# A planned decoder kernel: start loads, sample block, turned loops and planner model changed together

## The chip, the cores and the metric

The kernel runs as one program on the 8 cores of one Trainium2 chip: cores 0 to 3 are one die, 4 to 7 the other. The metric is the device time in microseconds (us) of the slowest core. Executions fall in a fast and a slow state; in the slow one the cores of a die show a lower granted TensorE clock (down to about 0.81 of full) and the time is some per cent, for the kernel before up to 18%, longer.

## The reference, cut to what matters

```python
def mixer_layer(h, p_i, ...):                       # 4 layers, D_MODEL = 1024, D_FF = 2816
    z = rmsnorm(h, g_mix) @ w_in                    # columns: A (xa, gate_b, gate_c), B (u, v), C (c_in)
    ...
    y_a = gate_b * causal_dwconv(gate_c * xa)       # 3 taps
    y_b = gelu(u) * chunk_spatial_mix(layernorm(gelu(v)))
    y_c = silu(layernorm(causal_dwconv(glu(c_in)))) # 31 taps
    h = h + concat(rmsnorm(y_a), rmsnorm(y_b), rmsnorm(y_c)) @ w_out
    f = rmsnorm(h, g_ffn)
    h = h + (silu(f @ w_gate) * (f @ w_up)) @ w_down
    gate = sigmoid(rmsnorm(h, g_ple) @ w_ple_gate)  # per-layer input embedding
    return h + gate * (p_i @ w_ple_proj)
```

Each core has one prompt of 2048 rows and 128 rows of samples. Four RMS norms a layer stand in the path of the matmuls: each needs the whole row's sum of squares before the first matmul behind it can have its input.

## The kernel before

The rows are worked through in two halves of 1024, each in two blocks of 512 columns; the sample block of 128 columns rides with the first half. So the four layers of the first half have three blocks and those of the second half two. A layer reads its weights from HBM anew in each half: wC, wV, wU, wA and wT for the mixing stage, wO for the output projection, wF and wD for the feed-forward pair, wP for the embedding.

The kernel is a graph of operations. A list scheduler fixes in advance, from a cost model, the order of the instructions on every engine, and also every address in SBUF.

```python
    for o in reversed(ops):                         # plan(): latest start D of each operation
        ...
        if o.dma:
            o.D = dend - (o.dma / 120.0 + 500)
        ...
            if o.dma:                               # two queues modelled as independent
                q = "sw" if e == "pool" else "hw"
                b0 = max(dmaf[q], t + o.cost + 900)
                dmaf[q] = b0 + o.dma / 125.0
                o.end = dmaf[q] + 1100
```

A norm: ScalarE squares the eight chunks of h into buffers SQ (two buffers of four chunks), VectorE or GpSimd adds them, TensorE sums over the partitions with a matrix of ones, ScalarE takes the root (RB), VectorE scales the eight chunks one by one into NRM.

```python
    def norm(H, bi, n, gcol, label="NRM", dt=BF16):
        bank = sumsq(H[bi], n)                      # SQ, additions, ones-matmul
        rb = rstd(bank, n, 1.0 / D)                 # RB
        dst = keys8(label, bi, n, dt)
        scale_by(H[bi], gcol, rb, dst, n)           # eight scalar_tensor_tensor, NRM
        return dst
```

The matmuls behind a norm take one PSUM bank at a time and all eight chunks for it, so the first of them waits for the last chunk:

```python
            for m in range(8):                      # wO; c_proj, wF and wP are built alike
                ps = G.psum(n)
                pe(n, mmg(lambda ps=ps: ps.ap, [(..., lambda k=MX[bi][kc]: k.ap) for kc in range(8)]),
                   [w] + MX[bi], (ps,))
                residual(bi, m, ps)
```

The order in which the parts of the mixing stage enter the graph is given by strings (Q = C projection, V, U, A, K, L, M = mixing, a, b, c = group norms; the last digit is the block), one for each half and one for the very first layer.

Of the kernel before, what the change touches and what calls it, by code (L numbers as in the profile page):

```python
# [11 lines left out]
DEPTH = 4  # L12
# [12 lines left out]
RING = 65536  # L25


SEQ = ("Q1 A00 Q2 Q0 A01 K0 A02 K1 V1 L0 V0 L1 A20 A12 B A10 U2 U0 c1 c0 M0 V2 L2 a0 c2 b0 A21 U1 A11 M1 a1 A22 M2 b2 b1 a2",
       "A00 V1 Q0 Q1 K1 A10 V0 K0 L1 U0 L0 A20 B A21 a0 M0 b0 c0 A01 U1 M1 c1 A11 b1 a1")
SEQ_FIRST = "R* K0 A0* B K1 M* L0 b0 A10 A20 c0 a0 L1 b1 A11 A21 c1 a1 L2 b2 A12 A22 c2 a2"  # L30
# [10 lines left out]
def c_pe(n):  # L41
    return max(n / 2.4 + 3.0, 58.0)
# [44 lines left out]
class Op:  # L87
    __slots__ = ("i", "eng", "cost", "fn", "deps", "raw", "succ", "tiles", "tset", "T", "D", "start", "end", "pos",
                 "dma", "sem", "val", "ndep", "est", "waits", "snap", "needed", "count", "wslab", "gate", "pre", "bg", "alt")


class Graph:
# [24 lines left out]
    def op(self, eng, cost, fn, r=(), w=(), tset=None, dma=0, gate=None, slab=None, bg=False, alt=None):  # L117
        o = Op()
        o.alt = alt or {}
# [33 lines left out]
    def plan(self, nunits, verbose=False):  # L153
# [9 lines left out]
        for o in reversed(ops):  # L163
# [16 lines left out]
            if o.dma:  # L180
                o.D = dend - (o.dma / 120.0 + 500)
            elif o.eng == "pe":
                o.D = min(o.T, dend - o.cost * 1.1)
            else:
                o.D = dend - o.cost * 1.3 - 100
# [7 lines left out]
        def takes(o, e, t):  # L193
# [5 lines left out]
            return t + o.alt[e][0] <= busy + o.cost  # L199
# [7 lines left out]
        dmaf = {"sw": 0.0, "hw": 0.0}  # L207
# [72 lines left out]
        while done < total:  # L280
# [4 lines left out]
            for e in ENGS:  # L285
# [3 lines left out]
                for o in ready[e]:  # L289
# [13 lines left out]
                    for tl in o.tiles:  # L303
                        if tl.at > a:
                            a = tl.at
                    cands.append((a, o))
# [81 lines left out]
            if o.dma:  # L388
                q = "sw" if e == "pool" else "hw"
                ft[e] = t + o.cost  # L390
                b0 = max(dmaf[q], t + o.cost + 900)
                dmaf[q] = b0 + o.dma / 125.0
                o.end = dmaf[q] + 1100
            else:
# [8 lines left out]
                o.end = t + c  # L403
            o.pos = len(order[e])
# [105 lines left out]
def build_program():  # L510
# [94 lines left out]
    def dve(n, fn, r, w, rate=1.0, ptr=0, flex=False, alt=None):  # L605
        alt = dict(alt or {})
        if flex:
            alt["pool"] = (c_pool(n), fn)
        return G.op("dve", c_dve(n, rate, ptr), fn, r, w, alt=alt)
# [10 lines left out]
    def load(out, in_, nbytes, w, gate=90000, r=()):  # L620
        return G.op("sp", 60, lambda e: e.dma_start(out=out(), in_=in_), r, w, dma=nbytes, gate=gate)
# [4 lines left out]
    def cast_load(out, in_, nbytes, w, gate=90000):  # L626
        return G.op("pool", 900, lambda e: e.dma_start(out=out(), in_=in_), (), w, dma=nbytes, gate=gate)

    def slab(label, src, n, after=()):
        k = Key(G, Tile(label, "w", n * 2), 0, n, BF16)  # L630
        G.op("pool", 600, lambda e: e.dma_start(out=k.ap, in_=src), after, (k,), dma=128 * n * 2, slab=k.tile)  # L631
# [7 lines left out]


    G.op("sp", 60, lambda e: e.dma_start(out=VECT[:], in_=vec), (), (kVEC,), dma=128 * NV * 4)
# [17 lines left out]
    def keys8(label, bi, n, dt):  # L659
        if n == 512:  # L660
# [61 lines left out]
    def ld_x(hf, blocks, bi, after=()):  # L722
# [3 lines left out]
        if kind == "S":  # L726
            load(lambda: G.whole(h).ap.rearrange("p (k t) -> p k t", k=8), xv[:, :, r0:r0 + n], 128 * n * 32, h)
# [5 lines left out]
    def layer(hf, l, blocks, H, NRM):  # L733
        nb = len(blocks)
        BI = range(nb)

# [13 lines left out]
        if hf == 0:  # L750
# [15 lines left out]


        kC = [slab("wC", wC[l, j], 2048) for j in range(2)]
        first = hf == 0 and l == 0
        kVl = []  # L770

        def wV_():
            if not kVl:
                kVl.append(slab("wV", wV[l], 3072, after=H[0] if first else ()))
            return kVl[0]
        if first:
            wV_()
            H[1] = ld_x(hf, blocks, 1, after=(kC[1],))
            NRM[1] = norm(H, 1, 512, lambda c: vcol(0, 0, c))
        wk = {}  # L780

        def wU_():
            if "U" not in wk:
                wk["U"] = slab("wU", wU[l], 3072)
            return wk["U"]
# [575 lines left out]
```

## Time and profile before

| | before |
|---|---|
| time, median of 4 runs | 3319.58 us |
| fast runs | 3318.25 to 3320.47 us |
| spans by core, profiled run | die 0 3310.2 to 3315.3 us, die 1 3293.7 to 3302.4 us |
| granted clock by core | 0.986 to 0.988 |
| core 2: TensorE idle | 3315.3 - 3163.3 = 152.0 us |
| core 2: first matmul of wO, first layer | 151.4 us |
| core 2: last layer of the first half, first wP matmul to the second half's first wO | 1712.3 to 1868.0, 155.7 us |

Columns of a list of what ended the idle time: us in total, times, longest.

```profile
PE PS L637 <- POOL SQ L689: 7.7, 3, 3.2
...
PE PS L637 <- DMA wO<-wO: 0.4, 1, 0.4
```

The wait for wO is there on all cores of die 0 (7.4 to 13.9 us) and nearly absent on die 1 (0 to 2.0 us). It is most of the 17 us between cores 2 and 7: their four stretches from the first wO to the first wF matmul in the second half add up to 135.0 and 120.6 us. That holds for this execution only. In the fast runs of the same kernel on two other chips, die 0 was the slower one in four of seven.

### The profile page before, as it was taken

How to read it: one execution, taken by the hardware profiler on the slowest of the kernel's cores; microseconds unless marked ns; L12 is line 12 of the kernel's file. 1: busy time of each engine (PE TensorE's matmuls, PEld its weight loads, DVE VectorE, ACT ScalarE, POOL GpSimd, SP SyncE). 2: the span in 40 equal slices, each digit the busy share in tenths (PEclk: the TensorE clock that was granted, in tenths of full speed). 3: DMA queues.
4: the chain of work that ended last, by engine and by line, in shares of the span. 5: the costliest groups of instructions: out<-in, count | busy, mean ns of one | idle time of the engine just before them, and what ended most of it. 6: DMA issues, size and time to landing. Idle time of an engine off the chain costs nothing.

```text
span 3315.3 us, 45695 instructions; the slowest of 8 cores (3293.7 to 3315.3 us)
## 1 busy us (share of the span) xinstructions
PE 3163.3 (95%) x18278; PEld 1549.7 (47%) x18278; DVE 1664.8 (50%) x2910; ACT 1182.8 (36%) x2052; POOL 537.0 (16%) x694
## 2 busy tenths in 40 slices
PE   4899999999999999999988899999999999999998
PEld 2455545555455554555544344444444444444443
DVE  4842179522696215972149721495117831386116
ACT  3631157311473113641125511363115621264114
POOL 4200033000331002310022200130002200031000
PEclk9999999999999999999999999999999999999999
DMA  9734545535365353753633745338443574428431
GB/s 176 117 64 71 87 69 99 102 55 88 57 113 92 59 89 59 117 87 62 124 70 95 114 82 100 67 49 139 83 85 70 83 122 89 81 48 131 79 58 51
DMA packets 75054, 288.78 MB, mean 87 GB/s; under 512 B 14304, under 2 KB 24672, under 8 KB 59488
## 3 DMA queue, kind: packets, MB, share of 16 engines
q0 software_dynamic: 47808, 255.09, 46.4%
q1 hardware_dynamic: 27040, 30.77, 3.1%
q8 instruction: 151, 2.47, 0.3%
q14 instruction: 55, 0.45, 0.1%
HBM read 529.55 MB, written 12.78 MB: 164 GB/s over the span
## 4 chain that ended last, share of the span: by engine, by line
PE 77%; DVE 14%; DMA 4%; ACT 2%; issue 2%; POOL 0%; SPq 0%; DVEq 0%; ACTq 0%; POOLq 0%
PE PS L637 77%; DVE NRM L709 2%; DMA wO<-wO 2%; DVE MX L709 1%; DVE TMP L1172 1%; DVE ACC L1028 1%; DVE H L1174 1%; DVE H L1112 1%; ACT SQ L666 1%; DMA nap<-XAP 1%; DVE TMP L1053 1%; DMA H<-xin 1%; DVE SQ L684 1%; DVE Y L951 0%; ACT L1206 0%
## 5 line engine op out<-in xcount | busy, mean ns | idle before, releaser
L637 PE MATMUL PS<-NRM,wF 128*128 128x512 bf16 x5632 | 1224.7, 379 | 3.5 <-DVE NRM L709 3.5
L637 PEld LDWEIGHTS PS<-NRM,wF 128*128 128x128 bf16 x5632 | 548.8, 98 | 657.6 <-issue 5.4
L1139 DVE TENSOR_TENSOR HID<-TMP,PS 128x512 bf16<-128x512 f32 x352 | 242.1, 688 | 930.8 <-PE PS L637 930.5
L637 PE MATMUL PS<-HID,wD 128*128 128x512 bf16 x2816 | 612.8, 379 | 0.0
L1137 ACT ACTIVATE TMP<-PS 128x512 f32<-128x512 f32 (+1 forms) x440 | 234.5, 533 | 1013.6 <-PE PS L637 1013.5
L666 ACT ACTIVATE SQ<-H 128x512 bf16<-128x512 f32 x416 | 253.0, 626 | 732.1 <-DVE H L1112 608.6
L637 PEld LDWEIGHTS PS<-HID,wD 128*128 128x128 bf16 x2816 | 274.7, 98 | 327.5
L1112 DVE TENSOR_TENSOR H<-H,PS 128x512 f32<-128x512 f32 x256 | 174.8, 685 | 479.9 <-PE PS L637 479.7
L709 DVE SCALAR_TENSOR_TENSOR NRM<-H,VEC,RB 128x512 bf16<-128x512 f32 x384 | 287.9, 803 | 18.1 <-ACT RB L670 17.7
L637 PE MATMUL PS<-NRM,wA 128*128 128x512 bf16 x1152 | 269.5, 388 | 3.0 <-DVE NRM L709 3.0
L637 PE MATMUL PS<-MX,wO 128*128 128x512 bf16 x1024 | 234.8, 389 | 10.4 <-DMA wO<-wO 7.4
L637 PE MATMUL PS<-NRM,wP 128*128 128x512 bf16 x1024 | 235.5, 381 | 9.2 <-DVE NRM L709 9.2
L1206 ACT ACT_TABLE_LOAD x162 | 207.8, 1283 | 2.5
L637 PEld LDWEIGHTS PS<-NRM,wA 128*128 128x128 bf16 x1152 | 112.9, 100 | 140.3 <-issue 14.7
L637 PEld LDWEIGHTS PS<-MX,wO 128*128 128x128 bf16 x1024 | 101.4, 100 | 137.5 <-issue 25.9
L637 PEld LDWEIGHTS PS<-NRM,wP 128*128 128x128 bf16 x1024 | 100.5, 98 | 130.9 <-issue 12.2
L637 PE MATMUL PS<-SQ,ONES 128*128 128x512 bf16 (+1 forms) x210 | 62.4, 359 | 93.6 <-DVE SQ L698 58.0
L631 POOL DMA_DIRECT2D wF<-wF x88 | 48.4, 552 | 591.0 <-PE PS L637 589.0
L631 POOL DMA_DIRECT2D wD<-wD x64 | 33.9, 532 | 672.6 <-PE PS L637 657.2
L637 PE MATMUL PS<-NRM,wC 128*128 128x512 bf16 x512 | 116.7, 385 | 7.1 <-DVE BST L873 7.1
L684 DVE TENSOR_TENSOR SQ<-SQ 128x1024 bf16<-128x1024 bf16 (+1 forms) x121 | 76.0, 632 | 61.8 <-ACT SQ L666 61.8
L1171 ACT ACTIVATE TMP<-PS 128x512 f32<-128x512 f32 (+1 forms) x160 | 82.5, 529 | 60.0 <-PE PS L637 59.3
(157 smaller groups left out, 2826.3 us busy)
## 6 DMA issues: line engine op xcount, KB each, us to landing
wF<-wF POOLq DMA_DIRECT2D x88, 1024.0 KB, 17.5
wD<-wD POOLq DMA_DIRECT2D x64, 704.0 KB, 7.3
wT<-tz POOLq DMA_DIRECT2D x32, 1024.0 KB, 10.9
wP<-wP POOLq DMA_DIRECT2D x32, 640.0 KB, 8.3
wA<-wA POOLq DMA_DIRECT2D x24, 768.0 KB, 10.3
wO<-wO POOLq DMA_DIRECT2D x32, 512.0 KB, 14.9
H<-xin SPq DMA_DIRECT2D x32, 256.0 KB, 7.4
wC<-wC POOLq DMA_DIRECT2D x16, 512.0 KB, 7.5
```

Of the source, the lines that this page charges most:

```text
L631: G.op("pool", 600, lambda e: e.dma_start(out=k.ap, in_=src), after, (k,), dma=128 * n * 2, slab=k.tile)
L637: return [(lambda e, i=i, l=l, r=r: e.matmul(out(), l(), r(), start=(i == 0), stop=(i == n - 1))) for i, (l, r) in enumerate(pairs)]
L666: act(n, lambda e: e.activation(dst.ap, src.ap, AF.Square), (src,), (dst,), )
L684: dve(2 * n, lambda e, sq=sq: e.tensor_tensor(two(sq, 0), two(sq, 0), two(sq, 2), ALU.add), sq, sq[:2], rate=0.5, flex=True)
L709: dve(n, lambda e, s=s, d=d, c=c: e.scalar_tensor_tensor(d.ap, s.ap, gcol(c), rb.ap, ALU.mult, ALU.mult), (s, rb, kVEC), (d,), ptr=1)
L1028: dve(n, lambda e, k=k: e.scalar_tensor_tensor(ac.ap, xall.ap[:, k * st_:k * st_ + n], vcol(l, 32, k * 3 + j), ac.ap, ALU.mult, ALU.add), ...
L1053: dve(n, lambda e, hp=hp, tm=tm, ps=ps: e.scalar_tensor_tensor(tm.ap.rearrange("p (a t) -> p a t", a=nt), ps.ap.rearrange("p (a t) -> p a ...
L1112: dve(n, lambda e: e.tensor_tensor(h.ap, h.ap, ps.ap, ALU.add), (h, ps), (h,))
L1137: act(n, lambda e, tm=tm, pg=pg: e.activation(tm.ap, pg.ap, AF.Silu), (pg,), (tm,), tset="silu", sb=False)
L1139: dve(n, lambda e, hd=hd, tm=tm, pu=pu: e.tensor_tensor(hd.ap, tm.ap, pu.ap, ALU.mult), (tm, pu), (hd,))
L1171: act(n, lambda e, tm=tm, pg=pg: e.activation(tm.ap, pg.ap, AF.Tanh, scale=0.5), (pg,), (tm,), tset="tanh", sb=False)
L1206: e.preload_act_table_set(o.pre)
```

## The change

The intent: shorten the start by loading first what is needed first; give the shorter half to the start and the longer to the rest; let TensorE begin as soon as one normed chunk is there; take the second half's first norms out of the way; and make the planner's model of DMA and of the port that VectorE and GpSimd share more truthful. The diff, cut to its core:

```diff
+DMA_RATE = 260.0
+FIRST_W = (3, 6, 7)
+LEAD = 'COFP'
+TAIL = 1
+AHEAD = ((0,), (1,))
+SMP = 1
-SEQ = ("Q1 A00 Q2 Q0 A01 ...", "A00 V1 Q0 Q1 ...")
-SEQ_FIRST = "R* K0 A0* B K1 M* ..."
+SEQ = ("Q1 B Q0 K0 V0 A00 U0 ...", "Q2 Q1 B Q0 A00 A01 V0 ...")
+SEQ_FIRST = "U0 Q0 Q1 V0 V1 K0 B A10 ..."
 ...                                              # planner
-                o.D = dend - (o.dma / 120.0 + 500)
+                o.D = dend - (o.dma / DMA_RATE + 500) - o.rank
-            return t + o.alt[e][0] <= busy + o.cost
+            return t + o.alt[e][0] + (600 if e == 'pool' else 0) <= busy + o.cost
+                    if e == "dve" and o.port and hold["pool"] > a:
+                        a = hold["pool"]
+                    elif e == "pool" and not o.dma and hold["dve"] > a:
+                        a = hold["dve"]
-                q = "sw" if e == "pool" else "hw"
-                b0 = max(dmaf[q], t + o.cost + 900)
-                dmaf[q] = b0 + o.dma / 125.0
+                b0 = max(dmaf, t + o.cost + 900)
+                dmaf = b0 + o.dma / DMA_RATE
-        G.op("pool", 600, ... dma=128 * n * 2, slab=k.tile)   # weight loads: bytes as written
+        G.op("pool", 600, ... dma=128 * n * 4, slab=k.tile)   # bytes as read
 ...                                              # turned loop
+    def groups(n, specs, xs, lead, order=range(8), done=()):
+        ks = list(order)
+        if not lead:
+            ...                                   # as before: one bank, all chunks
+        for i, kc in enumerate(ks):               # chunk kc into all four banks, then the next chunk
+            mms = [(lambda e, ps=ps, w=w, ...: e.matmul(ps.ap, w.ap[:, o:o + 128], k.ap,
+                    start=(i == 0), stop=(i == len(ks) - 1))) for ps, w, off in specs]
+            pe(n, mms, [w for _, w, _ in specs] + [xs[kc]], [ps for ps, _, _ in specs] + list(done))
 ...                                              # start
-    G.op("sp", 60, ... out=VECT[:], in_=vec ...)
+    G.op("sp", 60, ... out=VECT[:], in_=vec ..., rank=2e6)
+                aft = H[0][FIRST_W[len(wk)]:][:1] if first and len(wk) < len(FIRST_W) else ()
+                wk[x] = (... slab("wU", wU[l], 3072, after=aft) if x == "U" else ...)
+        if first:
+            H[1] = ld_x(hf, blocks, 1, after=H[0][7:8])
+            NRM[1] = norm(H, 1, 512, lambda c: vcol(0, 0, c))
+            late[:] = H[1][4:5]                   # small loads wait for this chunk
 ...                                              # blocks and halves
+    BLK = [[(0, 512, "P"), (512, 512, "P")] for _ in range(2)]
+    BLK[SMP].append((1024, 128, "S"))
+    def enter(hf, bi):                            # load x of a block and norm it
+        HH[hf][bi] = ld_x(hf, BLK[hf], bi)
+        NN[hf][bi] = norm(HH[hf], bi, BLK[hf][bi][1], lambda c: vcol(0, 0, c))
+    # in the last embedding stage of the first half: enter(1, x) for x in AHEAD[bi], ahead of block bi
```

## The prediction

> **What bounds the kernel now.** I read the page's first lines and the row of slices, then cut the span into stages, then looked at who ended TensorE's idle time in each. All of it is core 2, the slowest core of a fast execution; the dies are within 0.5% of each other.
>
> ```profile
> span 3315.3 us, 45695 instructions; the slowest of 8 cores (3293.7 to 3315.3 us)
> ...
> PE 3163.3 (95%) x18278; PEld 1549.7 (47%) x18278; DVE 1664.8 (50%) x2910; ACT 1182.8 (36%) x2052; POOL 537.0 (16%) x694
> ...
> PE   4899999999999999999988899999999999999998
> ...
> PEclk9999999999999999999999999999999999999999
> DMA  9734545535365353753633745338443574428431
> ```
>
> TensorE is the bound: 95% busy, 152.0 us idle. The change does not remove a matmul, so it can win only from that idle time and from the slow clock that follows it. The row of slices shows the idle time in three places: the first two slices, the middle, and the last. The stages, with columns span, PE, PEld, DVE, ACT, POOL busy, clock, DMA share, GB/s:
>
> ```profile
> 0.00:27.50 27.50, 0.01 (x1) 0.04 (x2) 3.14 (x5) 6.32 (x9) 15.45 (x25) 1.00 0.94 195
> 27.50:43.70 16.20, 6.58 (x45) 4.63 (x46) 13.82 (x28) 4.48 (x13) 6.29 (x12) 1.00 1.00 204
> 43.70:151.40 107.70, 85.35 (x627) 44.52 (x626) 81.51 (x161) 65.30 (x123) 38.45 (x51) 0.91 0.86 145
> ...
> 1707.00:1728.30 21.30, 8.88 (x107) 6.41 (x106) 16.93 (x19) 18.07 (x34) 12.10 (x10) 0.78 0.90 150
> 1728.30:1781.30 53.00, 41.51 (x238) 20.12 (x239) 49.91 (x86) 30.02 (x59) 18.50 (x17) 0.89 0.32 74
> 1781.30:1902.00 120.70, 107.98 (x644) 50.72 (x645) 98.61 (x170) 60.54 (x95) 26.96 (x31) 0.95 0.68 114
> 2195.00:2280.00 85.00, 77.55 (x513) 36.69 (x512) 72.36 (x121) 52.49 (x79) 18.22 (x23) 0.98 0.62 83
> 2575.00:2656.00 81.00, 74.09 (x434) 33.80 (x432) 69.30 (x113) 50.01 (x75) 16.72 (x20) 0.96 0.63 88
> 2950.00:3036.00 86.00, 76.66 (x486) 35.55 (x483) 70.18 (x116) 51.60 (x79) 17.69 (x22) 0.96 0.65 91
> 480.00:596.00 116.00, 110.75 (x844) 59.74 (x843) 110.89 (x227) 79.12 (x154) 41.15 (x51) 1.00 0.66 110
> ...
> 3299.40:3315.30 15.90, 1.01 (x2) 0.14 (x2) 9.92 (x15) 4.27 (x6) 1.99 (x2) 0.60 0.35 132
> ```
>
> The first output-projection matmul is issued at 151.4, after 59.5 us of idle. At the change of halves, 1707 to 1781, 23.9 us are idle. The mixing stage of a layer leaves 7 to 9 us idle with two blocks (second half) and about 5 with three (first half), where VectorE is busy 110.9 of 116 us. Between these stages, in the feed-forward layers, TensorE is busy 40.00 of every 40 us; there is nothing to win there. What ended the idle time, in the stretch 0:152 and then 1700:1800:
>
> ```profile
> PE PS L637 <- DVE SQ L698: 35.0, 3, 27.5
> PE PS L637 <- DVE BST L873: 7.1, 1, 7.1
> ```
> ```profile
> PE PS L637 <- DVE NRM L709: 12.3, 2, 9.2
> PE PS L637 <- DVE SQ L698: 10.0, 3, 4.6
> ```
>
> These are RMS norms: the sum of squares (SQ) and the normalised chunks (NRM). The start is really a DMA wait: the squares follow the eight loads of x one by one, the last at 24.79, and VEC, which every NRM needs, took 20.6 us to land.
>
> **What the Trainium skill says.** "TensorE: Matmul & The Clock Gate", What's actually happening: an idle window of about 3.4 us halves the clock until TensorE has been busy again. The trace agrees: after the 7.06 us gap at 64.7 and the 9.24 us gap at 1719 the clock in the table falls (0.91 and 0.78 over their stages). Idle time therefore costs more than itself. "SBUF — State Buffer", Who interferes with whom: a VectorE instruction with two SBUF inputs and a GpSimd instruction that reads SBUF block each other for the whole instruction. The trace agrees: NRM takes 747 ns in the median but up to 2928, and at 1718 to 1731, beside GpSimd's additions of squares (2.57 and 4.75 us in pieces), ten NRM take 12.70 us. "DMA: Bandwidth & Descriptors", Issuing engines are not separate DMA queues: both issuing queues share the same engines. The trace agrees at the start: with both in use the share is 0.94 to 1.00. The rate I use is from the trace: 195 GB/s over 24.8 us is about 4.8 MB as written, and as half of the weight and PT bytes are lost in the cast to bf16, about 6.6 MB as read, 0.278 MB/us.
>
> **The change, part by part.**
>
> 1. Start (new load order: VEC and x of block 0 first, weights after given chunks, small loads held back, the sample block out of the first half). VEC and x are 2.2 MB: 2.2 / 0.278 = 8 us, plus 1.5 us of issue and 2 us of latency: 11.5. A square 0.63, two additions 0.69 each, the sum on TensorE 1.0, the root 0.7: about 16. Eight NRM x 0.745 = 6 us: the first projection (U, not chunked) starts at 22 instead of 38.5 (sample) or 43.7 (block 0). Then DMA and TensorE race. A layer's mixing weights and wO are, by the sizes of the issue list doubled for fp32, 22.5 MB; with 4.2 of x, 1.1 of PT and 1 of small loads 28.8 MB, which is 104 us at the measured rate. TensorE has about 73 us for two blocks in that stage (per block C 6.8, V 5.2, U 5.1, A 15.4, conv and mix some 4), from 22 with 4 us of cold clock: 99, plus holes where slabs come late. I take the first wO matmul at 104. Before it was 151.4, of which about 9.7 us are the sample block's matmuls (128 x 58 ns, 8 of 160 ns, the mixing), which move to the second half and are not won. Gain 151.4 - 9.7 - 104 = 37 us.
>
> 2. Change of halves (AHEAD: the second half's x is loaded and normed while the last embedding stage of the first half runs). 23.9 us idle and, by the clock, 0.22 x 8.9 + 0.11 x 41.5 = 6.5 us of slow matmuls. With norms done early, each behind 17 us of matmuls, I leave 3: gain 27. The second half's first mixing stage (12.7 idle, 5.4 slow clock) comes with three blocks and a new order: I leave 6, gain 12.
>
> 3. LEAD in two-block layers: for the first groups of C, O, F and P the loop is turned so that four PSUM banks take chunk 0, then chunk 1, and so on; TensorE starts one NRM after the root instead of eight, saving up to 7 x 0.745 = 5.2 us of exposed wait per place, but only where TensorE stands there. It costs no matmul. The three layers lose 7.4, 6.9 and 9.3 us plus 0.02 x 77.6, 0.04 x 74.1 and 0.04 x 76.7 of clock: 31 us. I leave 3.5 each: gain 20. These layers are now in the first half.
>
> 4. Three-block layers: VectorE is within 5 us of full there, so a new order cannot do much; the port model removes some blocked NRM time, but GpSimd gets less work, which comes back at 0.68 us each. Gain 3.
>
> 5. End: the last block is now the sample block, so block 1's 16 us tail begins under its 80 small matmuls (4.6 us), and its own tail adds about 2: gain 3.
>
> Sum: 37 + 27 + 12 + 20 + 3 + 3 = 102 us. The plan fixes every engine's order in advance, and a plan that is newly good at one place usually meets a wait elsewhere; I take off 10 us for that: 92. **Predicted 3319.6 - 92 = 3228 us.**
>
> **The rivals.**
>
> - DMA bounds the start harder. Share 1.02 between 80 and 120 speaks for it; without the sample block TensorE has less work to hide the same bytes. If the rate falls to 0.24 the 28.8 MB take 120 us, the start wins only 21: 3244.
> - VectorE takes the wait's place. It was 110.9 of 116 us busy with three blocks, and norms made ahead in the embedding stage sit where it is already busy (49.9 of 53.0). Then parts 2 to 4 win half, about 31 less: 3259.
> - Lead backfires: four banks end together, and the next group waits for evacuation (a SiLU 597 ns, a multiply 688 ns). Eight banks exist, and one group of 32 matmuls is 6.8 us long, so I expect under 1 us a place: 15 us at most.
> - It goes all the way: 152 idle and about 40 of slow clock with only 22 + 6 at the start, 12 at the end and 3 a layer left: 3185.
>
> **Range and chances.** The rivals span 3185 to 3259, and two of them can come together; I take 3190 to 3268. Faster by 2% is below 3253: the sum has to lose over a quarter of its 92 us to miss it. Faster 0.81, within 2% 0.18, slower 0.01: nothing is added to TensorE, so slower needs a broken plan.
>
> **What would show it.** First real matmul near 22 and first wO near 104; PE busy down to about 3135 by the clock alone, with as many matmuls; no gap over 3 us near the change of halves; fewer GpSimd additions and NRM near 750 ns in the mean instead of 803; idle before wF, wP and wC from DVE NRM gone. I am wrong if the start still idles over 45 us, if the three-block stages of the second half grow longer than 116 us by more than the waits they shed, or if new waits on DMA of wT and wA appear in every layer.

## More of the kernel before

To read the stages of all kernels I use four marks a layer: the time of the first matmul with wO, wF, wD and wP. The stretch wF to wP is the feed-forward pair, where TensorE is always busy; wP to the next wO is the embedding plus the mixing of the next layer; wO to wF is the output projection plus the norm behind it. The last two hold all the idle time but that of the start and the end.

One thing the prediction's fences don't show: who ended TensorE's idle time in the two-block layers of the second half (2040 to 3250), core 2 and then core 7.

```profile
PE PS L637 <- POOL SQ L689: 8.1, 3, 3.4
PE PS L637 <- DMA wO<-wO: 7.4, 5, 3.1
...
PE PS L637 <- DVE NRM L709: 2.4, 3, 0.8
```

## The result, and the profile after

| | before | after |
|---|---|---|
| median of all runs | 3318.77 us (15 runs) | 3240.23 us (11 runs) |
| lowest | 3302.93 | 3234.78 |
| median span of die 0, die 1 (profiled run) | 3313.1, 3297.3 | 3230.7, 3233.8 |
| granted clock by core | 0.986 to 0.988 | 0.993 to 0.995 |
| TensorE idle (core 2 before, core 7 after) | 152.0 us | 3233.9 - 3145.9 = 88.0 us |
| mean of an NRM instruction of 512 columns, core 7 | 802 ns | 767 ns |

The ratio of the fast runs is 0.9771, 95% interval 0.9757 to 0.9784: faster by 2.3%. All ratios are the mean time of one kernel's fast runs over that of the other's of the same rounds, so not quite the ratio of the medians quoted.

The page of the kernel after, its slowest core (0). About 300 matmul records are missing from this core (x17965 against x18278), so its TensorE time reads too low, and I read stages from core 7, which has all of them.

```profile
span 3236.2 us, 45338 instructions; the slowest of 8 cores (3223.4 to 3236.2 us)
...
PE 3125.6 (97%) x17965; PEld 1548.9 (48%) x18278; DVE 1643.8 (51%) x2943; ACT 1159.0 (36%) x2036; POOL 487.2 (15%) x663
...
PE   6999999999999999999999999999999999999997
...
DMA  9745367434844356544763345643447343564321
```

The hole in the middle of TensorE's row is gone, the first slice is 6 where two slices were 4 and 8, and the end is 7 where it was 8. The stages of core 7 after: start, first mixing stage, change of halves, a three-block layer's embedding and mixing, end. Columns as in the prediction (span; PE, PEld, DVE, ACT, POOL busy; clock; DMA share; GB/s).

```profile
0.00:28.00 28.00, 1.01 (x2) 0.14 (x2) 8.23 (x17) 11.31 (x17) 6.79 (x22) 1.00 0.91 208
28.00:109.80 81.80, 77.73 (x512) 38.11 (x513) 63.40 (x110) 45.71 (x73) 29.47 (x39) 0.96 1.02 170
1475.70:1612.50 136.80, 124.07 (x834) 63.50 (x833) 131.09 (x240) 96.85 (x172) 50.26 (x56) 0.98 0.63 119
2750.10:2883.40 133.30, 124.86 (x913) 66.44 (x910) 124.19 (x241) 88.79 (x168) 57.04 (x64) 1.00 0.62 106
3176.40:3233.90 57.50, 40.88 (x251) 20.68 (x248) 45.09 (x93) 28.54 (x57) 7.28 (x7) 0.89 0.23 83
```

The same stages of core 2 before, cut at the same marks (its first mixing stage, 43.70 to 151.40, is among the lines in the prediction):

```profile
0.00:43.70 43.70, 6.59 (x45) 4.67 (x46) 16.96 (x33) 10.79 (x22) 21.74 (x36) 1.00 0.96 198
...
1712.30:1868.00 155.70, 122.09 (x767) 58.85 (x766) 138.95 (x231) 92.88 (x161) 54.92 (x53) 0.90 0.52 97
443.90:574.30 130.40, 125.07 (x913) 66.39 (x911) 122.99 (x234) 90.65 (x167) 52.67 (x63) 1.00 0.62 103
3263.70:3315.30 51.60, 36.70 (x167) 16.00 (x165) 41.01 (x60) 28.68 (x42) 6.71 (x5) 0.88 0.22 82
```

The first mixing stage is 26 us shorter and now runs with the DMA engines full (1.02 instead of 0.86). The change of halves has 12.7 us idle (136.8 - 124.1) where it had 33.6, with more matmuls in it. The three-block stage and the end have not become shorter.

The whole gain by stages, from the marks. The third and fourth columns count the sample block's matmuls out where they left (9.7 us at the start) and where they came in (5.1 at the change, 3.8 from wO to wF behind it, 4.6 at the end), so they compare like with like. Die 0 is what the metric saw before; die 1 shows what the change is worth where no wait for wO stood.

| term | predicted | core 2 before to core 7 after | core 7 before to core 7 after |
|---|---|---|---|
| start, to the first wO | 37 | 151.4 - 9.7 - 109.8 = 32 | 31 |
| change of halves and the second half's first mixing stage, to wF | 27 + 12 | 18.9 + 5.1 + 4.4 = 28 | 26 |
| two-block layers 2 to 4: wP to wO and wO to wF | 20 | 10.0 + 15.4 = 25 | 8.1 + 3.0 = 11 |
| three-block layers | 3 | -4 | -4 |
| end | 3 | -5.9 + 4.6 = -1 | -1 |
| discount | -10 | | |
| sum | 92 | 80 | 63 |

The spans differ by 3315.3 - 3233.9 = 81.4 and 3298.6 - 3233.9 = 64.7 us. So in these two executions some 16 us of the gain is that die 0 lost its lag: after the change the medians of the dies lie 3 us apart.

Who ended TensorE's idle time after, core 7, from 0 to 110:

```profile
PE PS L658 <- DVE SQ L732: 21.2, 1, 21.2
PE PS L658 <- DVE NRM L743: 6.4, 1, 6.4
PE PS L658 <- DVE SM L1007: 3.4, 1, 3.4
```

One block's norm is left at the start, and nothing else of size. (Lines have moved: L698, L709, L666 of before are L732, L743, L700.)

### The profile page after: what moved, and what is told of

It is laid out like the page before. It is cut to its first block, busy times and chain, and to the rows that moved or that the text cites. A ratio compares the mean times of both kernels' runs of the same rounds, so it can differ in the third digit from the quotient of the medians.

```text
span 3236.2 us, 45338 instructions; the slowest of 8 cores (3223.4 to 3236.2 us)
## 1 busy us (share of the span) xinstructions
PE 3125.6 (97%) x17965; PEld 1548.9 (48%) x18278; DVE 1643.8 (51%) x2943; ACT 1159.0 (36%) x2036; POOL 487.2 (15%) x663
## 4 chain that ended last, share of the span: by engine, by line
PE 80%; DVE 12%; ACT 5%; issue 2%; DMA 1%; POOL 0%; SPq 0%; DVEq 0%; ACTq 0%
PE PS L658 69%; PE PS L670 10%; DVE NRM L743 2%; ACT L1276 2%; ACT SQ L700 1%; DMA ncs<-GF 1%; DVE TMP L1215 1%; DVE H L1216 1%; DVE ACC L1066 1%; DVE H L1147 1%; DVE Y L988 1%; DVE GX L846 1%; DVE MX L743 1%; ACT RB L704 0%; DVE SQ L718 0%
## 5 line engine op out<-in xcount | busy, mean ns | idle before, releaser
L658 PEld LDWEIGHTS PS<-NRM,wF 128*128 128x128 bf16 x5120 | 499.3, 98 | 594.7
L1174 ACT ACTIVATE TMP<-PS 128x512 f32<-128x512 f32 (+1 forms) x440 | 232.6, 534 | 1014.3 <-PE PS L658 936.4
L700 ACT ACTIVATE SQ<-H 128x512 bf16<-128x512 f32 x416 | 252.0, 629 | 653.5 <-DVE H L1147 600.2
L743 DVE SCALAR_TENSOR_TENSOR NRM<-H,VEC,RB 128x512 bf16<-128x512 f32 x384 | 273.5, 768 | 46.9 <-ACT RB L704 46.9
L658 PE MATMUL PS<-NRM,wA 128*128 128x512 bf16 x1122 | 258.1, 384 | 1.7 <-issue 0.2
L1276 ACT ACT_TABLE_LOAD x148 | 189.9, 1283 | 2.3
L670 PE MATMUL PS<-NRM,wC 128*128 128x512 bf16 x499 | 114.9, 381 | 2.8 <-DVE NRM L743 1.6
L670 PE MATMUL PS<-NRM,wP 128*128 128x512 bf16 x501 | 114.9, 379 | 0.5
L658 PE MATMUL PS<-NRM,wP 128*128 128x512 bf16 x503 | 114.8, 379 | 0.5
L704 ACT ACTIVATE RB<-PS,EPSC 128x512 f32<-128x512 f32 (+1 forms) x125 | 75.9, 621 | 102.7 <-PE PS L658 101.8
```

Of the source, the lines that this page charges most:

```text
L658: return [(lambda e, i=i, l=l, r=r: e.matmul(out(), l(), r(), start=(i == 0), stop=(i == n - 1))) for i, (l, r) in enumerate(pairs)]
L670: mms = [(lambda e, ps=ps, w=w, o=off + kc * 128, k=xs[kc], i=i: e.matmul(ps.ap, w.ap[:, o:o + 128], k.ap, start=(i == 0), stop=(i == len( ...
L700: act(n, lambda e: e.activation(dst.ap, src.ap, AF.Square), (src,), (dst,), )
L704: act(n, lambda e: e.activation(rb.ap, bank.ap, AF.Abs_reciprocal_sqrt, bias=EPSC[:, 0:1], scale=inv_n), (bank, kEPS), (rb,), tset="rsqrt" ...
L743: dve(n, lambda e, s=s, d=d, c=c: e.scalar_tensor_tensor(d.ap, s.ap, gcol(c), rb.ap, ALU.mult, ALU.mult), (s, rb, kVEC), (d,), ptr=1)
L1174: act(n, lambda e, tm=tm, pg=pg: e.activation(tm.ap, pg.ap, AF.Silu), (pg,), (tm,), tset="silu", sb=False)
```

## The experiments

Twelve kernels ran, 1 to 4 on one chip, 5 to 8 on a second, 9 to 12 on a third. Each ratio is to the fast runs of the kernel before on the same chip in the same rounds; the kernel after has 0.9771. A difference in us between runs of different groups, or to the kernel after, crosses chips and is rough.

### 1. The turned groups turned back in the fixed order

```diff
+    for g in LG:                       # after the plan: the 64 turned groups
+        flat = [g[k].fn[s] for s in range(4) for k in range(8)]     # bank by bank again
+        ...                            # all chunks waited for once, evacuations follow their bank
```

> The changed kernel with its schedule kept (same buffers, same order of every other engine); only the 64 turned groups are turned back: each of the four PSUM banks takes its eight chunks in one go, after all eight are there, and is evacuated as soon as it is full. Theory A (the turned loop is what removed the waits between the norms and the output projection and feed-forward layers): the stretch from the first wO to the first wF matmul of a two-block layer goes from 28.7 back to about 33.5 us, the same in the three-block layers, in all 25 to 45 us: about 3275. Theory B (the new order of the stages did it; TensorE has other work while a norm is finished): under 10 us, 3240 to 3250.

Fast runs 3534.1 and 3535.9, ratio 1.0681: 294 us slower than after, 4.6 us for each of the 64 groups. No theory had this. That it is close to the up to 5.2 us that a turned group can save (seven NRM of 0.745 us) is chance: on core 7, TensorE idles 288.8 us where it idled 88.0 and its matmuls take 82.5 us longer at a lower mean clock, and 196 us of the idle time stand in front of ones-matmuls, the sums of squares, only 32 behind NRM. The edit also moves seven eighths of each turned group behind the ones-matmuls that stood between its chunks, so TensorE stands at a sum for which it used to have matmuls to fill the time. It shows that loop and order belong together, not what the loop is worth to a kernel that is planned without it. For that see 6 and 11.

### 2. Block 0's x alone on the DMA engines

```diff
+    kU.deps |= set(x0[:8])             # wU waits for all eight chunks of block 0
+    for o in x0[8:]:                   # x of block 1 waits for wU
+        o.deps |= {kU}
```

> The changed kernel with its schedule kept; only wU now waits for all eight chunks of x of block 0 (instead of the one named chunk, which the schedule loads first, so that it holds nothing back), and the x of block 1 waits for wU. Theory A (my term for the start was too good because x shared the DMA with wU and the next x: last square at 18.4 instead of 11.5): first U matmul at 22 to 23 instead of 28.6, the first wO matmul at about 104 instead of 109.8, the total 5 us less: 3235. Theory B (the whole first stage is bound by the bytes: DMA share 1.02 from 28 to 110 us): U starts earlier, but the first wO stays at 109 to 110 and the total within 1.5 us of 3240.

Fast runs 3243.5 and 3245.4, ratio 0.9803. The first U matmul came at 22.5, the predicted 22, but the first wO at 119.4 instead of 109.8. The first stage on core 7:

```profile
0.00:28.00 28.00, 6.53 (x16) 2.17 (x17) 8.61 (x17) 7.02 (x10) 5.69 (x20) 1.00 0.75 147
```

Where the kernel after moved 208 GB/s in these 28 us, this one moved 147: holding the rest back left the DMA engines partly idle, x of block 1 came late (33 to 42), and its ones-matmul stood in front of block 0's C projection in TensorE's order: TensorE idled 14.0 us for it, up to 44.5. What was won at U was lost twice over behind it.

### 3. The conv taps of group A cut to 32 columns (wrong on purpose)

```diff
-  e.scalar_tensor_tensor(ac.ap, xall.ap[:, k * st_:k * st_ + n], ...)
+  e.scalar_tensor_tensor(ac.ap[:, 0:32], xall.ap[:, k * st_:k * st_ + 32], ...)
```

> Wrong result on purpose: the two later taps of group A's convolution work on 32 columns instead of 512 or 128; the schedule is the same. It takes about 12 x 0.6 + 6 x 0.2 = 8.4 us of VectorE from a three-block layer and 7.2 from a two-block one, and nothing from TensorE. Theory A (VectorE bounds the three-block stages, which is why they won nothing): from wP to the next wO 131 to 133 us become about 126 (TensorE is busy 124 to 126 there), and the two-block stages move under 2 us (TensorE busy 108.8 of 109.8): in all about 20 us less, 3220. Theory B (chains of waits or ScalarE hold these stages): under 2 us a layer, 3232 to 3240.

Fast runs 3224.0 to 3226.7, ratio 0.9746. The result is wrong. VectorE's busy time between the first wP and the next wO matmul fell by 5.2, 5.8 and 7.7 us in the three-block layers (core 7; the 8.4 us of the expectation were an estimate), and wP to wO went from 130.6, 131.7 and 133.3 to 129.9, 129.2 and 130.3: 0.7 to 3.0 us. The theory that VectorE's throughput alone bounds these stages fell.

### 4. The kernel after with the old order strings, planned anew

```diff
-SEQ = ("Q1 B Q0 K0 ...", "Q2 Q1 B Q0 ...")
+SEQ = ("A00 V1 Q0 Q1 ...", "Q1 A00 Q2 Q0 ...")     # before's strings, halves exchanged
```

> The changed kernel with the order strings of the kernel before for layers after the first (the one for two blocks now used in the first half, the one for three blocks in the second); all else as changed, and the schedule made anew. Theory A (turned loop, early x and sample move carry the gain; the strings are fine tuning): at most 15 us worse, under 3256. Theory B (the strings are fitted to the rest, and most of what the two-block stages and the change of halves won is theirs): 40 us or more worse, 3280 to 3310, the loss being spread over the mixing stages.

Two fast runs, 3282.9 and 3284.1, where the fast runs of before on that chip gave 3308.6 to 3310.6: 45 to 50 us of the gain are lost. On core 7, wP to wO in the two-block layers is back at 115.2, 114.9 and 120.6 (after: 109.8, 110.9, 114.8; before: 113.2, 115.7, 114.7), the change of halves took 168.5 us (after 136.8), and wO to wF behind it 37.6 (after 33.0). But wO to wF in the two-block layers stayed at 28.4 to 29.2 (after 28.7 to 29.2). So the strings carry the first two, and the last is not theirs. The three-block layers took 421.9, 425.8 and 423.4 us from wO to wO, after 421.9, 424.0 and 425.0, before (core 2) 422.9, 423.2 and 423.0: none of the three orders moves that sum. Within it the old strings do move time: wP to wO was 125.9, 128.2 and 130.5 against 130.5, 131.7 and 133.3 after, and wO to wP was longer by as much.

### 5. The sample block in the first half as before, the rest as after

```diff
-SMP = 1
+SMP = 0                                 # with before's order strings, which are made for this
```

> The changed kernel with the sample block back in the first half and the order strings of the kernel before, the schedule made anew; turned loop, load order, early x, port model as changed. Theory A (moving the sample block is worth little by itself): two-block layers, now in the second half, take 28 to 29 us from the first wO to the first wF as they did with the old strings and the turned loop; total 3250 to 3275, nearer to the changed kernel than to the one before. Theory B (the move is what wins, at the start, the change of halves and the end): 3285 or more.

Fast runs 3251.6 and 3251.8, two more of 3271 with cores 4 and 5 disturbed; ratio 0.9846 with these in. Spans in the profiled run 3241.9 to 3250.3 us. Against before's fast runs of the same rounds (3310.6 to 3314.7) that is about 61 us. The two changes undone here, the sample block's move and the strings that are made for it, are together worth some 12 to 15 more: the kernel after ran on another chip, so this is rough. On core 7 the first wO comes at 136.3 and the change of halves takes 124.1. Against this run the kernel after gains 17 us at the start (136.3 - 9.7 - 109.8) and gives back 7.6 at the change of halves and 5 in the three-block layers. Experiments 6 and 9 to 12 take single parts from this kernel, as it plans more robustly.

### 6. As 5, no group turned, planned anew

```diff
-LEAD = 'COFP'
+LEAD = ''
```

> As e5, with no group turned, the schedule made anew (so that the order may adapt, which it could not in e1). Theory A (the turned loop is worth what the two-block stages showed, 5 us per two-block layer from wO to wF and little elsewhere): wO to wF back at 33 to 34 us in the two-block layers, total 20 to 30 us over e5. Theory B (the turned groups are worth what e1 showed, 4 to 5 us at each of 64 places, in any schedule): 100 us or more over e5. Theory C (the schedule finds other work): under 8 us over e5.

This one gives no usable total: on every run some cores were disturbed, the lowest was 3392.1, and the profiled run is slow. Cores 0 and 1 were undisturbed in three runs, at 3333 to 3342, about 90 us over the same cores in 5. On core 0, wO to wF in the two-block layers took 31.2, 30.5, 31.1 and 32.2 (5: 28.4 to 29.3), wP to wO 124 to 127 (5: 113 to 117). That is worse than before the change, which never turned a loop. In the two-block layers (2050 to 3285) TensorE waited 24.4 us for NRM, up to 7.5 at a time, where the kernel before waited 2.3 (core 7, 2040 to 3250). It is not that the new code frees its four banks late: the first wO bank of the layer at 2255.8 is full at 2259.0, and the addition that empties it starts at 2259.06. So without the turned loop the new plan leaves the norms open to view; what else hid them in the old plan isn't shown.

### 7. All other loads behind block 0's x

```diff
+    kU.deps |= set(x0[:8])
+    for o in x0[8:]:
+        o.deps |= set(x0[:8])
```

> The changed kernel with its schedule kept; wU and the x of block 1 both wait for the eight chunks of x of block 0, and then share the DMA (in e2 x of block 1 waited for wU as well, and the sum of its squares held up the C matmuls behind it). Theory A (landing of the first x is the term that was off): first U matmul at 23 to 26, the first wO 3 to 5 us earlier than 109.8, total about 3236. Theory B (bytes bound the stage; TensorE and DMA are balanced from 28 to 110): the first wO at 108 to 112, total within 2 us of 3240.

Fast runs 3247.4, 3273.6 and 3277.2 (the last two with cores 4 and 5 disturbed), ratio 0.986. U began at 25.7, the first wO came at 119.6. As in 2, TensorE stood at the ones-matmul of block 1, 11.6 us up to 44.0, as that x now landed up to 41.7. So 2 and 7 show what an earlier first norm costs in this fixed order of TensorE. A kernel planned anew with it was not tried.

### 8. The ones-matmuls one group later in TensorE's order

```diff
+        if s.bg and not x.bg and x.start - (s.start + s.cost) < 300:
+            q[i], q[i + 1] = x, s       # the next group first, then the sum of squares
```

> The changed kernel with buffers and every other engine's order kept; in TensorE's order each ones-matmul of a sum (squares or means) is put behind the group that followed it, so it is reached 0.9 to 1.9 us later. Theory A (the 6 to 7 us that TensorE still idles in a three-block stage are ones-matmuls reached before their squares are ready, TensorE taking its queue in order): three-block stages from wP to the next wO 2 to 4 us shorter, total 5 to 12 us less. Theory B (those sums are on the chain that leads to wO, so that the delay is paid at its end): three-block stages the same or up to 3 us longer, total 3240 to 3255.

Fast runs 3245.0 to 3272.3, ratio 0.9812; on core 7 the span was 3232.5 against 3233.9 after. wP to wO in the three-block layers stayed at 130.6, 130.8 and 133.4, wO to wF grew by a microsecond. A sum that stands too early in TensorE's queue is not what holds these stages.

### 9. As 5, without the early norms of the second half

```diff
-AHEAD = ((0,), (1,), ())
+AHEAD = ((), (), ())
```

> Against the run with the sample block first (fast 3251.6; on core 7 its change of halves, first P matmul of the last layer of the first half to first wO matmul of the second, took 124.1 us; before 155.7). Theory A: loading and norming the second half's x during the last embedding stage is what shortened it; with that taken away the change of halves goes back to 145-160 us and the whole run to 3272-3285. Theory B: turned loop and new planner order do it without the early norms: 124-132 us, and the run stays under 3260.

Ratio 0.9856, interval 0.9804 to 0.9908, where 5 has 0.9846. (Experiments 9 to 12 ran together on a chip where before's own fast runs gave 3325 to 3342, with die 1 disturbed, so their totals aren't held against the others'; ratios and single stages of undisturbed cores are. The ratios are blurred by that die. By the median span of die 0 the fast runs of 9, 10, 11 and 12 are about 11, 24, 36 and 42 us longer than those of 5; by the ratios, 3, 18, 25 and 34.) The change of halves took 123.6 us on core 1 and 125.0 on core 3, against 124.1 and 124.9 in experiment 5. Theory A fell: entering the second half's x ahead of time isn't what shortened the change of halves as a whole. At the border itself the early norms do what they were meant to do: without them TensorE waits 5.7 us there (core 3: 2.6 for a sum of squares, 3.0 for the first chunk), with them under 1; the stages around it shorten by as much. What 9 loses on die 0 stands mostly from wO to wF in the three-block layers (core 1: 35.4 to 36.0, in 5 33.0 to 33.3), which the edit doesn't touch. The section behind experiment 12 says what else held the change of halves.

### 10. As 5, with the old load order

```diff
-FIRST_W = (3, 6, 7)                     # also: rank of VEC, x of block 1 behind block 0, small loads held back
+FIRST_W = ()
```

> Against the run with the sample block first (fast 3251.6, first wO matmul at 136.3 on core 7; before 151.4). Theory A: the new load order (VEC and x first, weights behind given chunks) made those 15 us: first wO back at 148-153, run at 3264-3270. Theory B: the bytes bound the start whatever their order, and the turned loop and other planning made them: first wO stays at 134-140, run under 3258.

Ratio 0.9901, interval 0.9865 to 0.9936. On core 3 the first wO came at 146.2 against 138.0 in 5. That is between the two theories: the load order makes 8 us of the gain at the start in this kernel, and the rest of the 13 to 15 is left for turned loops and the planner. (The edit takes the new rules away; wV doesn't wait for x as it did in the old kernel.)

### 11. As 5, only the F groups turned back

```diff
-LEAD = 'COFP'
+LEAD = 'COP'
```

> Against the run with the sample block first (two-block layers, core 7: first wO to first wF 28.4-30.4 us, first P to next wO 112.3-116.6). Only the F groups (first feed-forward matrix) are turned back, and the order is planned anew. Theory A: the turned F loop is what shortened wO to wF by 4-5 us a layer: it returns to 31-34 in all four two-block layers and the three-block ones grow by 2 or more too, P to wO unchanged within 1.5, run at 3262-3285. Theory B: the schedule hides it otherwise: wO to wF stays under 30 in the two-block layers, run within 5 us of 3251.6.

Ratio 0.9922, interval 0.9874 to 0.9971. On core 3, wO to wF in the two-block layers went from 28.5, 29.2, 28.7 and 28.5 to 30.9, 34.7, 30.9 and 31.0, in the three-block layers from 34.0, 33.0, 33.3 and 33.0 to 35.3, 36.0, 37.1 and 38.4; wP to wO in the two-block layers stayed within 0.5. The wait is plain to see in the first two-block layer, TensorE's first matmul with wF (start, duration, engine, what; in brackets the idle time and who ended it):

```profile
1872.03 1.89 PE L658 MATMUL PS<-NRM,wF 128*128 128x512 bf16 x8 [2.31 <-DVE NRM L743]
```

Theory A is right in kind, and its 4 to 5 us a layer were too many: the turned loop at wF is worth 2.3 us of wait in a two-block layer, and more where the granted clock fell behind the wait (34.7: the mean clock in that stretch was 0.84). This is the cleanest measure of the turned loop: 26 us over eight layers for one of its four places, though here too the plan was made anew.

### 12. As 5, without the port model and the GpSimd penalty

```diff
-            return t + o.alt[e][0] + (600 if e == 'pool' else 0) <= busy + o.cost
+            return t + o.alt[e][0] + 0 <= busy + o.cost
-                    if e == "dve" and o.port and hold["pool"] > a:
-                        a = hold["pool"]
-                    elif e == "pool" and not o.dma and hold["dve"] > a:
-                        a = hold["dve"]
```

> Against the run with the sample block first (fast 3251.6; mean of the norm instruction 754 ns on core 7, 641 to 663 GpSimd instructions). The planner no longer knows of the VectorE-GpSimd port and has no penalty for giving work to GpSimd. Theory A: the model is worth something on the chip: norm mean back to 785-805 ns, waits of TensorE for it grow, run at 3260-3275. Theory B: TensorE's order hides those waits: norm mean grows but the run stays within 5 us of 3251.6.

Ratio 0.9948, interval 0.9906 to 0.999: against 5 that is 1% or 34 us lost, the largest loss of the four that ran together, though its interval and that of 11 overlap. But the way is not the one that theory A gave: the mean of an NRM went from 754 to 760 ns on core 7, not to 785. GpSimd had 704 instructions instead of 641, busy for 557 us instead of 455 (core 3), and TensorE's losses are spread out: wO to wF in three-block layers 35.1 instead of 33, wP to wO in two-block layers 118.5, 114.5 and 116.5 instead of 116.7, 112.7 and 113.1, the change of halves 132.9 instead of 124.9.

### What the change of halves was waiting for

Experiment 9 left the question. The answer is in ScalarE's order. In the kernel before, core 7, ScalarE from 1663 to 1714 (start, duration, what; in brackets the idle time before and who ended it):

```profile
1668.69 0.31 ACT L666 ACTIVATE SQ<-HS 128x128 bf16<-128x128 f32 x1 [4.94 <-DVE HS L1112]
1706.36 5.84 ACT L666 ACTIVATE SQ<-H 128x512 bf16<-128x512 f32 x11 [37.35 <-PE PS L637]
1712.21 1.28 ACT L1206 ACT_TABLE_LOAD   x1
1713.51 0.69 ACT L670 ACTIVATE RB<-PS,EPSC 128x512 f32<-128x512 f32 x1
```

ScalarE stood for 37.35 us and then did eleven squares in a row. What it squared had long been there: VectorE had written h of block 0, and x of the second half was requested at 1577 to 1626. What was missing was room. In the plan the buffer of these squares lies on memory of HID, the hidden rows of the feed-forward pair, which the wD matmuls of block 1 read to the end; those end at 1706.2 (the first matmul of the sample block's wD is issued at 1706.16), and the squares start 0.2 us later. They belong to the norms in front of wP. It is thus the norm of the last layer of the first half whose squares came 37 us late, and TensorE waited for it at the first wP matmuls. Its waits on core 7 from 1626 to 1760:

```profile
PE PS L637 <- DVE NRM L709: 9.3, 1, 9.3
PE PS L637 <- DVE SQ L698: 5.5, 2, 3.2
```

Of these, 12.5 us are for the norm in front of wP (3.2 and 9.3); the other 2.2, at 1753, are for a sum of the output norm. And the address made only part of the 12.5. When the squares came at last, GpSimd was adding squares just while VectorE made the eight NRM of block 0 (same core, timeline of 1680 to 1732):

```profile
1717.24 12.71 DVE L709 SCALAR_TENSOR_TENSOR NRM<-H,VEC,RB 128x512 bf16<-128x512 f32 x10
1720.68 4.75 POOL L684 TENSOR_TENSOR SQ<-SQ 128x1024 bf16<-128x1024 bf16 x2 [0.30 <-ACT SQ L666]
1727.56 4.66 PE L637 MATMUL PS<-NRM,wP 128*128 128x512 bf16 x11 [9.29 <-DVE NRM L709]
```

Taken one by one, four of those eight NRM took 1.15, 2.61, 2.61 and 2.60 us, each beside an addition on GpSimd, where the others took 0.74 or 0.75: 6 us of the 9.3. That is the blocking which the prediction read from the same lines, and in the kernel after none of the eight is longer than 0.75.

In the kernel after, core 7, the squares come one at a time behind each chunk of h, and the root at 1462.56 is 13 us ahead of the first wP matmul (1475.68):

```profile
1447.68 0.63 ACT L700 ACTIVATE SQ<-H 128x512 bf16<-128x512 f32 x1 [4.12 <-DVE H L1147]
...
1456.46 4.79 ACT L700 ACTIVATE SQ<-H 128x512 bf16<-128x512 f32 x9 [3.40 <-PE PS L658]
...
1462.56 0.69 ACT L704 ACTIVATE RB<-PS,EPSC 128x512 f32<-128x512 f32 x1
```

The kernels whose plan differs can be put beside each other (1, 2, 3, 7 and 8 keep the plan of the kernel after): how long ScalarE stood at most between the first wD matmul of that layer and some 20 us after the first wP matmul, and how long TensorE then waited there for squares and NRM.

| kernel | ScalarE stood | TensorE waited | turned loop |
|---|---|---|---|
| before | 37.35 | 12.5 | no |
| 6, no group turned | 37.36 | 10.7 | no |
| 10, old loads | 37.35 | 4.5 | yes |
| 12, no port model | 37.35 | 4.6, 3.6 of it put down to a load of wT | yes |
| 4, old strings | 22.39 | none over 0.5 | yes |
| 11, F not turned | 18.36 and 16.80 | 3.7 | C, O and P only |
| 9, no early norms | 12.40 | none over 0.5 | yes |
| 5, and after | under 12 | 0.7 at most | yes |

The 3.6 us of 12 stand in front of the same first wP matmul, just behind its first NRM, as the 3.5 us of 10 do, so I count them. So ScalarE's long stand is an address: the plan puts the squares on memory that comes free late, and everything on ScalarE stands in order behind it. The plan itself means it so. `plan()` needs no chip; run by itself for the kernel before, it has the inputs of the first of these squares ready at 1657.2 and starts it at 1689.6, as HID is released, 37.4 us after ScalarE's last work. At 1657 it had 118 of its 132 memory units in use, 44 by HID and 22 by x of the second half, which had been let in early in this kernel too. Memory was short, and early x helped to fill it. Nothing in the change aims at this. Whether the plan lands there depends on all of it (parts 6, 10 and 12 each bring it back, 9 doesn't), and where it does, the turned loop at wP leaves less of the wait (4.5 and 4.6 us in 10 and 12, 10.7 in 6), as TensorE can begin at the first late NRM. The Trainium skill, "Perfetto Trace Analysis", Tensor Engine Instruction, says that ScalarE, VectorE and GpSimd are strict FIFOs; the trace agrees, with 37.35 us for it. What I did not try is to forbid the plan that memory and change nothing else, so the address as the cause is read from the plan and the release times, not shown by an experiment of its own.

## Why the prediction was right or wrong

The time on record was 3228 with a range of 3190 to 3268; 3240.23 is within it, and "faster by over 2%" came true with little room (2.3%). Of the 92 us of the sum 80 were measured on the die that set the time before, 63 on the other; that the total came so near is in part luck, as terms missed on both sides.

1. **Start, predicted 37, measured 32.** The step that failed is the first norm: U at 22, measured 28.6. The sum behind it took x of block 0 to have the DMA engines to itself. It has not: the chunk that releases wU (the fourth) is loaded first, so wU is issued at 5.84 and x of block 1 from 7.96, and the last squares of block 0 start 18.43, not near 12. Core 7 after, three lines of the first 30 us:

```profile
5.84 0.73 POOL L652 DMA_DIRECT2D wU<-wU  x1 [2.23 <-DMA H<-xin]
...
18.43 1.19 ACT L700 ACTIVATE SQ<-H 128x512 bf16<-128x512 f32 x2 [5.08 <-DMA H<-xin]
...
28.63 7.38 PE L658 MATMUL PS<-NRM,wU 128*128 128x512 bf16 x24 [6.40 <-DVE NRM L743]
```

   The second term was right: from U to wO I had 104 - 22 = 82 us, measured are 109.8 - 28.6 = 81.2, with DMA at 1.02 and TensorE busy 77.7 of 81.8. There is another reading. The prediction's rate has a slip: 6.6 MB in 24.8 us are 0.266 MB/us, not 0.278, and at 0.266 its 28.8 MB take 108 us, whatever U does. That speaks for the rival "DMA bounds the start harder" in kind, at a third of its 16 us. The record doesn't separate the two: experiments 2 and 7 moved U forward and lost 10 us, but to TensorE's fixed order (14.0 and 11.6 us at one ones-matmul), so that the missed 6 us could not have been had isn't shown.

2. **Change of halves, predicted 27 + 12, measured 28.** Of the 39 us 28 came, and the reason was in part wrong. I put the 23.9 us of idle time there down to the second half's x, normed too late. About half of it, 12.5 us on core 7, was the norm before wP of the layer that ended, its squares held up by an address and its NRM by GpSimd; only 7.6 us (4.6 and 3.0, 1777 to 1781) stood in front of the second half's first matmuls. Experiment 9 takes the early norms away, gets 5.7 us of wait back at that place, and its stage is no longer. The step "with norms done early I leave 3" failed, and with it the 12 for the stage behind it: 12.7 us are idle in the stretch after, where I had left 3 + 6. TensorE's longest waits there, core 7, 1460 to 1620:

```profile
PE PS L658 <- DVE SQ L732: 5.0, 2, 4.4
PE PS L658 <- DVE SM L1007: 2.2, 1, 2.2
```

3. **Two-block layers, predicted 20, measured 25 on die 0 and 11 on die 1.** I had read the idle time as waits for NRM that the turned loop would take away. NRM was 2.4 us of it. The larger ones were the additions of squares on GpSimd (8.1 us; none after, and the penalty for GpSimd work is what the planner has against them, though no run takes it out alone) and, on die 0 alone, wO coming late (7.4 us). The turned loop does its share (experiment 11: 2.3 us a layer at wF alone), and the new strings theirs (experiment 4: 5 us a layer). That die 0 stopped waiting for wO I had not foreseen; it accounts for most of the difference between the dies. The traces say how: the kernel before asked for the four loads of wO 11.0 to 9.3 us ahead of the first wO matmul in the last three layers, and the fourth landed 12 to 14 us behind it (core 2; on core 7 about 10); the kernel after asks 44 to 38 us ahead, and all have landed 12 us ahead. Experiments 4, 5, 6, 9, 10, 11 and 12 ask at least 23 us ahead in these layers and don't wait for wO either, without the new strings, the move, the turned loop, the early norms, the load order or the port model, one or two at a time. That leaves the planner's new model of DMA (one queue, bytes as read) as the likely cause; no run takes it out.

4. **Three-block layers, predicted 3, measured -4.** The mechanism, VectorE within 5 us of full, is refuted as the only bound by experiment 3: 5.2 to 7.7 us less work, 0.7 to 3.0 us won. What the chain of work through the end of such a stage shows (core 7 after, 1985 to 2040, shares by line) is TensorE for 57.7% and then ScalarE, its table loads as much as its squares:

```profile
by line: PE PS L658 48.5%; PE PS L670 9.2%; ACT L1276 7.0%; ACT SQ L700 6.7%; issue 5.5%; DVE Y L988 3.5%; ACT Y L938 3.1%; POOL Y L1021 2.7%; PE PS L1086 2.1%; ACT Y L1022 1.5%; DVE ACC L1066 1.3%; DVE YS L1019 1.3%; DVE SM L1007 1.2%; POO
```

   A dependent chain over several engines, then. Experiment 4 shortens the stage itself by 2.8 to 4.6 us with the old strings and loses as much from wO to wP, so an order of stages alone shifts the wait. Which link would shorten the whole is open.

5. **End, predicted 3, measured -1.** "Block 1's tail begins under the sample block's 80 matmuls" failed: TensorE's busy time grew by 4.2 us (36.70 to 40.88) and its idle time from 14.9 to 16.6. The sample's matmuls were added to the tail and hid none of it.

6. **The discount**, 10 us for waits that a new plan meets elsewhere, can't be measured by itself: the terms above fall short of their 102 us by 22. Its reason was sound: experiments 6, 9, 10, 11 and 12 each shift waits of 2 us and more into stages that their edit doesn't touch.

Of the signs: the matmul count is the same and TensorE's busy time is 3145.9 (predicted 3135); no gap over 3 us near the change of halves is wrong (4.4 us is left); NRM near 750 ns is half right (767, and 754 in experiment 5); fewer GpSimd instructions is right (663 for 694). The start idles 32 us, under the 45 that would have spoken against it. The rivals at 3259 (VectorE in the wait's place) and 3185 (it goes all the way) did not come; the turned loops did not backfire.

No correct variant was faster than the kernel after; experiment 3 is, but its result is wrong.

## What to carry to other kernels

When the engine orders and addresses are planned in advance, ask of a long wait not only which data it lacked but which memory: an instruction whose inputs are long ready and that starts the moment some other engine finishes reading is waiting for its own output buffer, and in an in-order queue it holds up all behind it. Then look at what fills the memory: data that was let in early takes room too. Turning a loop so that four accumulators share each arriving chunk is worth the most where an input arrives in pieces right in front of it, and it also leaves less of a wait for pieces that come late for other reasons. An edit to a planned kernel re-plans everything, so measure a part against the stages it can touch, on undisturbed cores, before crediting it with the total.

## What the Trainium skill lacked or had wrong

- "TensorE: Matmul & The Clock Gate", Seeing it yourself, gives 13/16 of the clock as what a die gets once three of its cores run dense matmuls, and advises to count on that for kernels on all cores. Here all eight cores run dense matmuls, and in the profiled executions of the kernels before and after and of experiment 5, all fast, the granted clock was 0.986 to 0.996. About 0.81 appeared in some executions (0.812 and 0.813 on die 0 in one run of experiment 11, at 3885.9 us, while die 1 had 0.966 to 0.969). The number agrees; that it is the normal case does not.
- "ScalarE: Activation LUTs", What ACT_TABLE_LOAD costs, gives 1283 ns for the load plus a drain of about 1380 ns for each switch. The load agrees (1.28 us); the drain isn't seen: before the change, core 7, the eleven squares end at 1712.20, the load starts at 1712.21, and the next function starts at 1713.51, 1.30 us after the load's start.
- "Perfetto Trace Analysis", Optimization Strategy, gives too little SBUF or PSUM as a possible reason for a gap that repeats on the engine that should be saturated. It doesn't tell of a single such wait on another engine. Here one was 37.35 us on ScalarE, once, listed in the profile under the engine that last read the memory, and TensorE waited up to 12.5 us behind it.
- No page tells of a difference between dies in how late a weight load lands: 7.4 to 13.9 us of TensorE's waits for wO on the cores of die 0 and 0 to 2.0 us on those of die 1, in one execution of one program.
